# The first 60 microseconds of a transformer layer: vector work to GpSimd, loads in another order

## The chip, the core and the metric

The kernel runs on one core of a Trainium2 chip. The core has a matrix engine (TensorE, PE in the profile), a vector engine (VectorE, DVE), a scalar engine (ScalarE, ACT), a general engine (GpSimd, POOL) and a queue that issues the loads and stores (SyncE, SP). The metric is the device time of one execution in microseconds (us), and lower is better.

## The reference: one layer

One layer on a sequence of 1024 tokens of 1024 features. What matters here is the first product, `h = x @ w_in`, whose columns are cut into queries, keys, values and gates:

```python
h = x @ w_in[l]                       # (1024, 1024) @ (1024, 5120)
qa, ka, va, qb, kb, vb, ga, gb = jnp.split(h, split_pts, axis=-1)
y_a = chunk_band_attention(heads_a(qa), heads_a(ka), heads_a(va), rel_bias[l]) @ w_proj_a[l]
y_b = stick_breaking_attention(heads_b(qb), heads_b(kb), heads_b(vb)) @ w_proj_b[l]
mix = (gate_a * y_a + gate_b * y_b) @ w_out[l]
x = layer_norm(DEEPNORM_ALPHA * x + mix, ln1_g[l], ln1_b[l])
g, u = jnp.split(x @ w_ffn_in[l], 2, axis=-1)
x = layer_norm(DEEPNORM_ALPHA * x + (jax.nn.silu(g) * u) @ w_ffn_out[l], ln2_g[l], ln2_b[l])
```

All values are float32, and the result is held to float32 accuracy. The kernel reads x transposed (`xt`: features by tokens) and `w_in` cut into column blocks of 128, each stored as a 128 x 1024 tile.

## The kernel before

**Split operands.** A factor is cut into a high part, rounded to the matrix engine's fast float32 form (`F32R`), and a low part, the rest. A product takes three matmuls: high by high, high by low, low by high (`mm3`, line 112, and `product`, line 159). `split` (line 108) makes both parts: ScalarE casts the high part, VectorE subtracts it from the source for the low one. In the profile both stand at lines 109 and 110, whatever tile they make.

**Seven products for eight.** Two column blocks of weights, left and right, are projected together as a work unit. Unit 0 is done plainly (`project_plain`, line 301): four blocks of 24 matmuls, left and right weights by the first half of the tokens (columns `LO` of each x tile), then by the second (`HI`). Each block goes over the 8 x tiles. Later units use a Strassen-like scheme (`pair_steps`, line 174) of seven half-size products, 12 matmuls each, in the order p1, p2, p6, p5, p7, p3, p4. p1 and p2 read x's first half, p4 its second half, p6 and p3 the halves of the tiles `s24`, p5 and p7 the halves of `s13`. `s13` and `s24` are sums of parts of x (lines 266 to 275), made once for four pairs of x tiles (`kt` 0 to 3) and split themselves. The weights of a unit need combinations too: `prep_left` (line 128) loads and splits the left tile, `prep_right` (line 139) loads the right one, forms `ta` and `tb` and splits them, and `prep_last` (line 153) splits a half of the right one into the tile `c`.

**Order of the work.** `run_pairs` (line 377) first issues p1 and p2 of units 1 and 2, then the remaining five products of unit 1, and so on; weights of later units are prepared between. So on TensorE the beginning is: four plain blocks of unit 0, p1 and p2 of unit 1, p1 and p2 of unit 2, then p6, p5, p7, p3, p4 of unit 1.

**Before the first products** (lines 239 to 275) the left weights of unit 0 are loaded, then the first halves of the eight x tiles in the order 0, 4, 1, 5, 2, 6, 3, 7, and split; then the right weights of unit 0, two second halves of x, the left weights of unit 1, and the other six second halves. All subtractions and all sums are VectorE's. GpSimd has no work there but a few memsets.

**Buffers and queues.** Tiles have tags with a fixed number of buffers (`SLOTS`, line 43): three for raw weights (`gt`), four for scratch and sums (`kp`), eight for split weights (`op`). A tile that asks for a buffer in use waits for its last reader. All loads go through the one queue of SyncE. A planner at compile time ranks the instructions of each engine by their place in the program and by when it thinks that they are ready, so that the order on an engine can differ a little from the program's; once made, each engine's order is fixed, and the instructions wait on semaphores.

The steps that the prediction speaks of: `split` and `split_w` (lines 108, 133), `left`, `right` (lines 232, 235), the loads and splits (lines 239 to 265), the sums (266 to 275), `project_plain` (301), and `right(1)` at line 429.

Of the kernel before, what the change touches and what calls it, by code (L numbers as in the profile page):

```python
# [11 lines left out]
F32 = mybir.dt.float32  # L12
# [6 lines left out]
P = 128  # L19
# [28 lines left out]
def hybrid_trunk_kernel(ctx: ExitStack, tc, x, xt, w_in, b_gate, rel_bias, w_proj,  # L48
# [14 lines left out]
    def slot(tag, name, dtype=F32):  # L63
        return pool.tile([P, 1024], dtype, tag=tag, name=name, bufs=SLOTS[tag])
# [40 lines left out]
    s_dr = [[dram(f"s_dr{g}_{hf}_", 7) for hf in range(2)] for g in range(4)]  # L105
    rel_dr = dr.tile([8, 896], F32, name="rel_dr")

    def split(dst_h, dst_l, src):
        nc.scalar.copy(dst_h, src)  # L109
        nc.vector.tensor_tensor(dst_l, src, dst_h.bitcast(F32), ALU.subtract)  # L110

    def mm3(acc, pairs):
        n = len(pairs)
# [19 lines left out]
    def split_w(raw, nm, tag):  # L133
        h = slot(tag, f"{nm}h", F32R)
        l = slot(tag, f"{nm}l", F32R)
        split(h, l, raw)
        return h, l

    def prep_right(W, nm, src, tag, tag_a=None):
        sub = ALU.subtract  # L140
        L = W["L"]
        R = W["R"] = slot("gt", f"wR{nm}")
        dma(R, src)
        ta = slot("kp", f"ta{nm}")
        tb = slot("kp", f"tb{nm}")
        nc.vector.tensor_tensor(ta[:, LO], R[:, LO], L[:, LO], sub)
        nc.vector.tensor_tensor(tb[:, LO], R[:, HI], ta[:, LO], sub)
        nc.vector.tensor_tensor(tb[:, HI], L[:, HI], tb[:, LO], sub)
        W["hb"] = split_w(tb, f"wb{nm}", tag)
        nc.vector.tensor_tensor(ta[:, HI], R[:, HI], R[:, LO], sub)  # L150
        W["ha"] = split_w(ta, f"wa{nm}", tag_a or tag)

    def prep_last(W, nm, tag):

        c = slot(tag, f"wc{nm}", F32R)
        split(c[:, LO], c[:, HI], W["R"][:, HI])
        W["c"] = c
# [74 lines left out]
    def left(i):  # L232
        prep_left(Wa[i], f"p{i}", w_in[work[i][2]])

    def right(i):
        prep_right(Wa[i], f"p{i}", w_in[work[i][3]], "op")
        prep_last(Wa[i], f"p{i}", "kp")

    sops = {}
    s_tags = iter(["bw"] * 9 + ["pt"] * 4 + ["yt"] * 3)  # L240
    for kt in range(4):
        for nm in ("s24", "s13"):
            sops[nm, kt] = tuple(slot(next(s_tags), f"{nm}{p}{kt}", F32R) for p in "hl")
    order_k = [0, 4, 1, 5, 2, 6, 3, 7]
    xraw = [None] * KT
    for k in order_k:
        xraw[k] = cycle(QKV, f"xraw{k}")
    left(0)
    for k in order_k:
        dma(xraw[k][:, LO], xt[k * P:(k + 1) * P, LO])  # L250
    xh = [slot("xt", f"xh{k}", F32R) for k in range(KT)]
    xl = [slot("xt", f"xl{k}", F32R) for k in range(KT)]
    for k in order_k:
        split(xh[k][:, LO], xl[k][:, LO], xraw[k][:, LO])

    R0 = slot("gt", "wRp0")
    dma(R0, w_in[work[0][3]])
    Wa[0]["hr"] = split_w(R0, "wrp0", "op")
    for k in order_k[:2]:
        dma(xraw[k][:, HI], xt[k * P:(k + 1) * P, HI])  # L260
    left(1)
    for k in order_k[2:]:
        dma(xraw[k][:, HI], xt[k * P:(k + 1) * P, HI])
    for k in order_k:
        split(xh[k][:, HI], xl[k][:, HI], xraw[k][:, HI])
    for kt in range(4):
        a, b = xraw[kt], xraw[kt + 4]
        s13 = slot("kp", f"s13_{kt}")
        s24 = slot("kp", f"s24_{kt}")
        nc.vector.tensor_tensor(s13[:, LO], a[:, HI], b[:, HI], ALU.add)  # L270
        nc.vector.tensor_tensor(s24[:, LO], s13[:, LO], a[:, LO], ALU.subtract)
        nc.vector.tensor_tensor(s24[:, HI], b[:, LO], s24[:, LO], ALU.subtract)
        nc.vector.tensor_tensor(s13[:, HI], a[:, LO], a[:, HI], ALU.subtract)
        for src, nm in ((s24, "s24"), (s13, "s13")):
            split(*sops[nm, kt], src)

    def s_op(nm, half):
        return [tuple(t[:, half] for t in sops[nm, kt]) for kt in range(4)]
# [22 lines left out]
    def project_plain(i):  # L301

        W, pair = Wa[i], work[i][1]
        accs = {}
        for half in (LO, HI):
            for side, key in enumerate(("hl", "hr")):
                tag = "pv" if side and half == HI else "tr"
                acc = accs[side, half.start] = bank(tag, f"plain{side}_{half.start}")
                wh, wl = W[key]
                mm3(acc, [(wh[:, k * P:(k + 1) * P], wl[:, k * P:(k + 1) * P],  # L310
                           xh[k][:, half], xl[k][:, half]) for k in (0, 4, 1, 5, 2, 6, 3, 7)])
        def take():
            for side, (scale, d) in enumerate(((-0.125, q_dr), (1.0, k_dr))):
                h = cycle(QKV, f"hi{side}_{i}", F32R)
                t = cycle(QKV, f"lo{side}_{i}")
                for half in (LO, HI):
                    acc = accs[side, half.start]
                    nc.scalar.activation(h[:, half], acc, AF.Copy, scale=scale)
                    nc.vector.scalar_tensor_tensor(t[:, half], acc, scale,
                                                   h[:, half].bitcast(F32),  # L320
                                                   ALU.mult, ALU.subtract)
                store_hl(d[pair], h, t)
        return take
# [102 lines left out]

    left(2)
    take = project_plain(0)
    right(1)
    take()  # L430
    run_pairs([project(i) for i in range(1, len(work))], lambda i: left(i + 1) if i > 1 else None,
              lambda i: right(i + 1), lambda i: small_inputs() if i == 2 else None)
# [692 lines left out]
```

## Time and profile before

| | us |
|---|---|
| median of three runs | 1466.01 |
| lowest and highest of them | 1466.0 and 1467.67 |
| the profiled execution's own time | 1465.81 |
| its span (first to last instruction) | 1464.0 |
| TensorE busy in the span | 1432.2 |
| VectorE busy | 1025.3 |
| ScalarE busy | 679.4 |
| GpSimd busy | 278.1 |

A row of the timeline has the start and the length in us, the engine, the line of the kernel, the operation, the tile written and those read, the shape, and in brackets the idle time of the engine before it and what ended that. A row of the groups has, behind the bar, the busy time in us and the mean length of one instruction in ns. Instructions on one engine overlap a little at their ends: the row of a 512-wide VectorE instruction is 0.69 us long, but the next one starts 0.60 us after it.

### The profile page before, as it was taken

How to read it: one execution, taken by the hardware profiler on the slowest of the kernel's cores; microseconds unless marked ns; L12 is line 12 of the kernel's file. 1: busy time of each engine (PE TensorE's matmuls, PEld its weight loads, DVE VectorE, ACT ScalarE, POOL GpSimd, SP SyncE). 2: the span in 40 equal slices, each digit the busy share in tenths (PEclk: the TensorE clock that was granted, in tenths of full speed). 3: DMA queues.
4: the chain of work that ended last, by engine and by line, in shares of the span. 5: the costliest groups of instructions: out<-in, count | busy, mean ns of one | idle time of the engine just before them, and what ended most of it. 6: DMA issues, size and time to landing. Idle time of an engine off the chain costs nothing.

```text
span 1464.0 us, 19115 instructions
## 1 busy us (share of the span) xinstructions
PE 1432.2 (98%) x6740; PEld 1184.4 (81%) x6740; DVE 1025.3 (70%) x1637; ACT 679.4 (46%) x1179; POOL 278.1 (19%) x326
## 2 busy tenths in 40 slices
PE   8999999999999998999999999999999999999997
PEld 6788888887888787878888888888888888888886
DVE  8856655434776876887848966777776665978767
ACT  6444444335878878775413534444444433221201
POOL 0000000003555879760004100000000000100016
PEclk9999999999999999999999999999999999999999
DMA  6565545338666476856611123444444457887602
GB/s 216 158 188 173 157 145 177 124 99 249 188 196 206 131 217 184 238 179 247 232 43 72 50 95 130 158 154 148 152 151 145 152 195 247 301 308 235 213 15 101
DMA packets 83455, 247.72 MB, mean 169 GB/s; under 512 B 10512, under 2 KB 10512, under 8 KB 83360
## 3 DMA queue, kind: packets, MB, share of 16 engines
q1 hardware_dynamic: 83360, 246.51, 51.5%
q8 instruction: 53, 0.87, 0.3%
q14 instruction: 42, 0.34, 0.1%
HBM read 162.03 MB, written 80.77 MB: 166 GB/s over the span
## 4 chain that ended last, share of the span: by engine, by line
PE 86%; DVE 5%; DMA 3%; ACT 3%; issue 2%; POOL 1%; SPq 0%; POOLq 0%; DVEq 0%; ACTq 0%
PE sxf L171 16%; PE sxp L171 12%; PE szf L171 8%; PE dx L1058 6%; PE szp L171 6%; PE syf L171 4%; PE gps L421 3%; PE dz L1058 3%; PE syp L171 3%; PE yAps L630 2%; PE ops L117 2%; PE ops L119 2%; PE ops L116 2%; PE fpswh_h L119 1%; PE fpswh_h L116 1%
## 5 line engine op out<-in xcount | busy, mean ns | idle before, releaser
L1014 POOL TENSOR_TENSOR wdyt<-wdyt 128x512 f32<-128x512 f32 x8 | 10.8, 1352 | 513.6 <-DMA wdgt<-in_w_ffn_out_dram 429.1
L547 POOL TENSOR_TENSOR w_b<-w_b,kp_b 128x511 f32<-128x511 f32 (+3 forms) x96 | 96.2, 1010 | 39.0 <-DVE kp_b L542 27.0
L542 DVE TENSOR_TENSOR_SCAN kp_b<-kp_b,ident_ps 128x512 f32<-128x512 f32 (+2 forms) x64 | 56.4, 883 | 24.8 <-ACT kp_b L539 24.3
L482 POOL MEMSET bias<- 64x64 f32 x8 | 1.2, 144 | 329.7 <-ACT bias L481 329.7
L778 POOL TENSOR_TENSOR mv<-mv,neghalf 128x1 f32<-128x1 f32 x16 | 23.8, 1489 | 210.3 <-DVE mv L777 210.3
L184 DVE TENSOR_TENSOR c<-sxp,c 128x512 f32<-128x512 f32 x16 | 11.1, 691 | 74.2 <-issue 41.1
L539 ACT ACTIVATE kp_b<-sc_b 128x512 f32<-128x512 f32 (+3 forms) x96 | 50.0, 521 | 24.9 <-PE sc_b L465 23.2
L110 DVE TENSOR_TENSOR pt_b<-tp_b,pt_b 128x512 fp32r<-128x512 f32 (+1 forms) x96 | 50.4, 543 | 13.8 <-ACT pt_b L109 13.5
L989 DVE TENSOR_TENSOR x<-dx,x 128x512 f32<-128x512 f32 x64 | 43.5, 686 | 17.0 <-PE dx L1058 16.9
L171 PE MATMUL szf<-x1S63h,wcf 128*128 128x512 f32 x168 | 55.1, 389 | 0.0
L109 ACT CAST pt_b<-tp_b 128x512 fp32r<-128x512 f32 (+1 forms) x96 | 48.2, 515 | 7.7 <-PE tp_b L570 6.1
L110 DVE TENSOR_TENSOR sl<-h,sl 128x512 fp32r<-128x512 f32 x56 | 38.4, 685 | 18.8 <-ACT sl L109 18.8
L512 POOL TENSOR_SCALAR w_a<-w_a,st_a 128x640 f32<-128x640 f32 (+2 forms) x64 | 42.6, 670 | 45.1 <-DVE st_a L511 33.5
L109 ACT CAST sl<-h 128x512 fp32r<-128x512 f32 x56 | 34.7, 619 | 34.5 <-PE syf L171 17.1
L110 DVE TENSOR_TENSOR pt_a<-tp_a,pt_a 128x512 fp32r<-128x512 f32 (+1 forms) x96 | 45.8, 486 | 6.8 <-ACT pt_a L109 5.5
L540 ACT ACTIVATE w_b<-sc_b 128x511 f32<-128x511 f32 (+3 forms) x96 | 50.2, 523 | 0.0
L570 PE MATMUL tp_b<-ident,w_b 128*128 128x128 f32 x288 | 48.7, 279 | 1.5 <-DVE pt_b L110 1.1
L116 PE MATMUL ops<-wh_o,mh 128*128 128x512 f32 x128 | 50.2, 392 | 0.0
L119 PE MATMUL ops<-wh_o,ml 128*128 128x512 f32 x128 | 50.0, 391 | 0.0
L117 PE MATMUL ops<-wl_o,mh 128*128 128x512 f32 x128 | 49.9, 390 | 0.0
L109 ACT CAST pt_a<-tp_a 128x512 fp32r<-128x512 f32 (+1 forms) x96 | 39.7, 426 | 19.2 <-PE tp_a L570 17.8
L507 ACT ACTIVATE w_a<-w_a,st_a 128x640 f32<-128x640 f32 (+2 forms) x64 | 44.7, 698 | 6.4 <-DVE st_a L501 5.9
(1883 smaller groups left out, 4811.4 us busy)
## 6 DMA issues: line engine op xcount, KB each, us to landing
s_dr<-sl SPq DMA_DIRECT2D x112, 256.0 KB, 2.1
sd<-s_dr SPq DMA_DIRECT2D x56, 512.0 KB, 4.5
wLf<-in_w_ffn_in_dram SPq DMA_DIRECT2D x22, 512.0 KB, 4.3
wRf<-in_w_ffn_in_dram SPq DMA_DIRECT2D x22, 512.0 KB, 3.6
wLp<-in_w_in_dram SPq DMA_DIRECT2D x17, 512.0 KB, 5.4
wRp<-in_w_in_dram SPq DMA_DIRECT2D x17, 512.0 KB, 4.2
v_dr<-v SPq DMA_DIRECT2D x16, 512.0 KB, 4.6
qs<-q_dr SPq DMA_DIRECT2D x16, 512.0 KB, 5.3
```

Source lines behind the costliest of these rows:

```text
L109: nc.scalar.copy(dst_h, src)
L110: nc.vector.tensor_tensor(dst_l, src, dst_h.bitcast(F32), ALU.subtract)
L116: mm(acc, lh, rh, start=(i == 0), stop=False)
L117: mm(acc, lh, rl, start=False, stop=False)
L119: mm(acc, ll, rh, start=False, stop=(i == n))
L171: mm(acc, lw[:, ks], rx, start=(first and kt == i == 0), stop=(kt == 3 and i == 2), skip_group_check=not first)
L539: nc.scalar.activation(kp[:, c0:e], sc[:, 0:n], AF.Sigmoid, scale=-1.0)
L540: nc.scalar.activation(be[:, m0:e], sc[:, m0 - c0:n], AF.Sigmoid)
L542: nc.vector.tensor_tensor_scan(kp[:, 0:e], kp[:, 0:e], ident_ps()[:, 0:e], 0.0, ALU.mult, ALU.add)
L547: nc.gpsimd.tensor_tensor(be[:, m0:e], be[:, m0:e], kp[:, m0 - 1:e - 1], ALU.mult)
L570: tr(tp[:, (qb - lo_q) * P:(qb - lo_q + 1) * P], wt[qb - q0][:, (kb - qb) * P:(kb - qb + 1) * P], ident)
L1058: mm(acc, a, b, start=(first and i == n == 0), stop=(i == n - 1 == 1), skip_group_check=not first)
```

## The change

It touches the beginning and the helpers that it uses.

1. `split` can be given the engine that subtracts. `right` can leave its last step, the tile `c`, to a new `right_last`.
2. TensorE multiplies a tile of zeros five times (128 x 256, float32) into a bank that nothing reads, ahead of everything else.
3. The left weights of unit 0 come in two halves, the first ahead of x's first two tiles, the second behind them. x's first half comes in the order 0 to 7, and `project_plain` takes the tiles in that order for the first half of the tokens.
4. The right weights of unit 0 come ahead of x's whole second half, and the left and right weights of unit 1 behind it. The right weights are split in halves: the low part of the first half on VectorE, of the second half on GpSimd.
5. The low parts of x's second half are all GpSimd's (8 instructions of 128 x 512).
6. Of each `s13` and `s24` the first halves stay VectorE's, and the second halves, sums and low parts, go to GpSimd (4 instructions of 128 x 512 for each `kt`). Splits of these tiles are made by halves, so ScalarE has two casts for each one before.
7. The combinations of unit 1's right weights (`right(1, False)`) stand ahead of the sums in the program; before they stood behind the first products. The tile `c` stays behind them.

```diff
-    def split(dst_h, dst_l, src):
+    def split(dst_h, dst_l, src, eng=None):
         nc.scalar.copy(dst_h, src)
-        nc.vector.tensor_tensor(dst_l, src, dst_h.bitcast(F32), ALU.subtract)
+        (eng or nc.vector).tensor_tensor(dst_l, src, dst_h.bitcast(F32), ALU.subtract)
...
-    def right(i):
+    def right(i, last=True):
         prep_right(Wa[i], f"p{i}", w_in[work[i][3]], "op")
+        if last:
+            right_last(i)
+
+    def right_last(i):
         prep_last(Wa[i], f"p{i}", "kp")
...
     order_k = [0, 4, 1, 5, 2, 6, 3, 7]
+    warm = cst.tile([P, 256], F32, name="warm")
+    nc.vector.memset(warm, 0.0)
+    warm_ps = bank("mm", "warm")
+    for _ in range(5):
+        mm(warm_ps[:, 0:256], warm[:, 0:P], warm, start=True, stop=True)
+
     xraw = [None] * KT
     for k in order_k:
         xraw[k] = cycle(QKV, f"xraw{k}")
-    left(0)
-    for k in order_k:
-        dma(xraw[k][:, LO], xt[k * P:(k + 1) * P, LO])
     xh = [slot("xt", f"xh{k}", F32R) for k in range(KT)]
     xl = [slot("xt", f"xl{k}", F32R) for k in range(KT)]
+    L0, R0 = slot("gt", "wLp0"), slot("gt", "wRp0")
+    for key, t in (("hl", L0), ("hr", R0)):
+        Wa[0][key] = slot("op", f"w{key}h", F32R), slot("op", f"w{key}l", F32R)
+
+    def x_in(ks, cs):
+        for k in ks:
+            dma(xraw[k][:, cs], xt[k * P:(k + 1) * P, cs])
+
+    dma(L0[:, LO], w_in[work[0][2]][:, LO])
+    x_in((0, 1), LO)
+    dma(L0[:, HI], w_in[work[0][2]][:, HI])
+    x_in(range(2, 8), LO)
+    dma(R0, w_in[work[0][3]])
+    x_in(order_k, HI)
+    for ks, cs in ((range(4), LO), (range(4, 8), HI)):
+        split(*(t[:, cs] for t in Wa[0]["hl"]), L0[:, cs])
+        for k in ks:
+            split(xh[k][:, LO], xl[k][:, LO], xraw[k][:, LO])
+    for cs, eng in ((LO, nc.vector), (HI, nc.gpsimd)):
+        split(*(t[:, cs] for t in Wa[0]["hr"]), R0[:, cs], eng)
     for k in order_k:
-        split(xh[k][:, LO], xl[k][:, LO], xraw[k][:, LO])
-
-    R0 = slot("gt", "wRp0")
-    dma(R0, w_in[work[0][3]])
-    Wa[0]["hr"] = split_w(R0, "wrp0", "op")
-    for k in order_k[:2]:
-        dma(xraw[k][:, HI], xt[k * P:(k + 1) * P, HI])
+        split(xh[k][:, HI], xl[k][:, HI], xraw[k][:, HI], nc.gpsimd)
     left(1)
-    for k in order_k[2:]:
-        dma(xraw[k][:, HI], xt[k * P:(k + 1) * P, HI])
-    for k in order_k:
-        split(xh[k][:, HI], xl[k][:, HI], xraw[k][:, HI])
+    right(1, False)
+    put = nc.vector.tensor_tensor
+    put2 = nc.gpsimd.tensor_tensor
     for kt in range(4):
         a, b = xraw[kt], xraw[kt + 4]
         s13 = slot("kp", f"s13_{kt}")
         s24 = slot("kp", f"s24_{kt}")
-        nc.vector.tensor_tensor(s13[:, LO], a[:, HI], b[:, HI], ALU.add)
-        nc.vector.tensor_tensor(s24[:, LO], s13[:, LO], a[:, LO], ALU.subtract)
-        nc.vector.tensor_tensor(s24[:, HI], b[:, LO], s24[:, LO], ALU.subtract)
-        nc.vector.tensor_tensor(s13[:, HI], a[:, LO], a[:, HI], ALU.subtract)
-        for src, nm in ((s24, "s24"), (s13, "s13")):
-            split(*sops[nm, kt], src)
+        put(s13[:, LO], a[:, HI], b[:, HI], ALU.add)
+        put(s24[:, LO], s13[:, LO], a[:, LO], ALU.subtract)
+        put2(s24[:, HI], b[:, LO], s24[:, LO], ALU.subtract)
+        put2(s13[:, HI], a[:, LO], a[:, HI], ALU.subtract)
+        for nm, src, cs, eng in (("s24", s24, LO, nc.vector), ("s13", s13, LO, nc.vector),
+                                 ("s13", s13, HI, nc.gpsimd), ("s24", s24, HI, nc.gpsimd)):
+            split(*(t[:, cs] for t in sops[nm, kt]), src[:, cs], eng)
...
-                           xh[k][:, half], xl[k][:, half]) for k in (0, 4, 1, 5, 2, 6, 3, 7)])
+                           xh[k][:, half], xl[k][:, half])
+                          for k in (range(KT) if half == LO else order_k)])
...
-    right(1)
+    right_last(1)
     take()
```

## The prediction

> **What bounds the kernel now.** I read the page first (busy shares), then the chain of waits in the first 75 us, then the timelines of TensorE, VectorE and GpSimd there, and last GpSimd's rows late in the kernel, because the early trace does not show what the change asks of GpSimd. Page:
>
> ```profile
> span 1464.0 us, 19115 instructions
> PE 1432.2 (98%) x6740; PEld 1184.4 (81%) x6740; DVE 1025.3 (70%) x1637; ACT 679.4 (46%) x1179; POOL 278.1 (19%) x326
> ```
>
> TensorE (PE) is the bound and is idle for 1464.0 - 1432.2 = 31.8 us in all. So a change of the beginning can win only what TensorE waits or runs slowly there, and any delay there stays, since TensorE has almost nothing later in which to catch up. TensorE's timeline, each row with its wait in brackets:
>
> ```profile
> 5.81 0.80 PE L116 MATMUL plain<-xh,wlp0h 128*128 128x512 f32 x1 [5.81 <-ACT xh L109]
> 12.01 0.63 PE L116 MATMUL plain<-xh,wlp0h 128*128 128x512 f32 x1
> 12.44 0.63 PE L117 MATMUL plain<-xl,wlp0h 128*128 128x512 f32 x1
> 13.20 0.40 PE L116 MATMUL plain<-xh,wlp0h 128*128 128x512 f32 x1
> 13.43 0.40 PE L117 MATMUL plain<-xl,wlp0h 128*128 128x512 f32 x1
> 15.28 0.39 PE L116 MATMUL plain<-xh,wrp0h 128*128 128x512 f32 x1
> 20.74 0.39 PE L116 MATMUL plain<-xh,wlp0h 128*128 128x512 f32 x1
> 26.18 0.39 PE L116 MATMUL plain<-xh,wrp0h 128*128 128x512 f32 x1
> 44.25 0.50 PE L171 MATMUL sxp<-s24h,wbp1h 128*128 128x512 f32 x1 [0.93 <-ACT wbp1h L109]
> 45.51 0.50 PE L171 MATMUL sxp<-s24h,wbp1l 128*128 128x512 f32 x1 [0.53 <-DVE wbp1l L110]
> 48.74 0.50 PE L171 MATMUL sxp<-s13h,wap1h 128*128 128x512 f32 x1 [0.68 <-ACT c L197]
> 57.04 0.39 PE L171 MATMUL sxp<-xh,wbp1h 128*128 128x512 f32 x1
> ```
>
> The four plain blocks of 24 matmuls (left and right weights with x's first half, then with its second) start at 5.81, 15.28, 20.74 and 26.18. Until 12.44 the matmuls start 0.43 us apart (12.44 - 12.01), after that 0.23 (13.43 - 13.20): the half-speed start. A full-speed block takes 5.45 us (20.74 - 15.28), the first took 9.47. The product of work unit 1 that reads the last sum (p3) ends at 57.04; that time is my yardstick. The chain of waits (start, length, who) shows what sets the time between the plain blocks and there:
>
> ```profile
> 18.36 0.68 DVE xl L110
> 24.45 0.60 DVE s L271
> 25.06 1.14 DVE s24l L110
> 42.44 0.68 DVE tbp L148
> 44.26 1.20 DVE wbp1l L110
> 45.51 2.58 PE sxp L171 x10
> ```
>
> From 18.36 to 45.5 the chain is nearly all VectorE (DVE). The view by stages (stretch, its length, then busy us and count of PE, PEld, DVE, ACT, POOL) has it full and GpSimd (POOL) empty:
>
> ```profile
> 30.00:35.00 5.00, 5.00 (x23) 4.13 (x22) 5.00 (x8) 2.35 (x3) 0.00 (x0) 1.00 0.41 86
> ```
>
> Its 512-wide instruction costs 0.60 us, its 1024-wide one 1.14. The three waits at 44.25 to 48.74 (0.93 + 0.53 + 0.68 = 2.1 us) are its price so far.
>
> **The change part by part.** *Loads.* The bytes are the same, in another order. The rows of the scalar engine (ACT) that end on a landing:
>
> ```profile
> 8.99 3.33 ACT L109 CAST xh<-xraw 128x512 fp32r<-128x512 f32 x5 [0.69 <-DMA xraw<-in_xt_dram]
> 12.98 1.05 ACT L109 CAST wrp0h<-wRp 128x1024 fp32r<-128x1024 f32 x1 [0.66 <-DMA wRp<-in_w_in_dram]
> 15.62 1.05 ACT L109 CAST wlp1h<-wLp 128x1024 fp32r<-128x1024 f32 x1 [0.55 <-DMA wLp<-in_w_in_dram]
> ```
>
> The right weights land at 12.98 behind the left ones and x's first half, and do so again. Between 12.98 and 15.62, four pieces of 256 KB (two of x, one left weight) landed, 0.66 us each. After the change x's second half comes from 13.6 to about 18.3, unit 1's left weights at about 19.6 and its right ones at 20.9 (before: left at 15.62). On the DMA queue (SP) unit 2's left weights now wait for the right weights' buffer, which GpSimd's subtract frees at about 16; they are needed after 36, so this costs nothing unless they came 14 us late.
>
> *Weights in halves and zeros first.* The first cast is half as long and the first load 256 KB instead of 512, so the first real matmul can start near 4.9 instead of 5.81. The zero matmuls have no row before. By the count of columns five of 256 cost at least 5 x 0.21 = 1.1 us (half of 0.43), at most 5 x 1.12 = 5.6 (twice 0.279 for a 128-wide float32 transpose, twice again for the half-speed clock):
>
> ```profile
> L570 PE MATMUL tp_b<-ident,w_b 128*128 128x128 f32 x288 | 48.7, 279 | 1.5 <-DVE pt_b L110 1.1
> ```
>
> ```profile
> 0.71 0.20 POOL masks.py:197 MEMSET ident<- 128x128 f32 x1 [0.29 <-POOLq L1115]
> ```
>
> A memset stands ahead of them; with the first such rows at 0.71 I start them at 1.2, and they end between 2.3 and 6.8. I take 4.6 (five of 0.169 x 4; 0.169 is the group's busy time over its count, scaled in the same way): in time. If they run to 6.8, block 1 starts 2 us later but still meets the next limit. That limit is the last piece of x's first half: the five casts from 8.99 end at 12.32, its subtract follows at about 12.9, its last matmuls at 13.4. The right weights' first half is cast by 13.6. So block 2 starts at about 13.7 instead of 15.28, and this part gains 1.6 us at most, nothing if the clock stays low (8 x 3 x 0.43 = 10.3 us from 4.9 is 15.2). [...]
>
> *Half of the vector work to GpSimd.* This decides. Moved are 25 subtracts of 128x512: 1 of the right weights, 8 lows of x's second half, and per sum tile pair 4 (two sums, two lows) x 4. VectorE loses 25 x 0.60 = 15 us. All 25 read two SBUF operands, and so does nearly everything that VectorE keeps here. GpSimd's queue is empty in this stretch, so nothing of its own stands behind them; VectorE's queue does. ACT gets ten 1024-wide casts as twenty 512-wide ones, 10 x (2 x 3.33/5 - 1.05) = 2.8 us over some 45 us, in which it is about half idle: nothing. How VectorE and GpSimd stand beside each other is shown late in the trace, at lines 1014 and 110:
>
> ```profile
> 1244.85 1.29 POOL L1014 TENSOR_TENSOR wdyt<-wdyt 128x512 f32<-128x512 f32 x1 [9.07 <-PE fpswh_h L119]
> 1303.67 1.63 POOL L1014 TENSOR_TENSOR wdyt<-wdyt 128x512 f32<-128x512 f32 x1 [14.66 <-DVE wdgt L1013]
> ```
>
> ```profile
> 1244.63 0.68 DVE L1072 SCALAR_TENSOR_TENSOR x<-x,fpswh_h 128x512 f32<-128x512 f32 x1
> 1245.22 1.45 DVE L110 TENSOR_TENSOR wdc<-wdyt,wdc 128x512 fp32r<-128x512 f32 x1
> 1303.45 0.69 DVE L110 TENSOR_TENSOR wdc<-wdyt,wdc 128x512 fp32r<-128x512 f32 x1
> ```
>
> VectorE's subtract of two SBUF tiles that began during GpSimd's took 1.45 us instead of 0.69, and ended at 1246.67, 0.53 after GpSimd's end at 1246.14. In the other order GpSimd took 1.63 instead of 1.29 and ended at 1305.30, 1.16 after VectorE's end at 1304.14. The instruction with a PSUM operand (1244.63) was not held. So such instructions go one at a time: a GpSimd one holds the pair for 1.16, a VectorE one for 0.53 to 0.60, and 25 moved instructions add 25 x 1.16 = 29.0 to what 25 x 0.60 = 15.0 took before. [...]
>
> *The sum.* From 13.6, when the first half of the right weights is cast, until p3's last matmuls, the pair must do: VectorE 22 of 0.60 (1 right weights, 4 of unit 1's combinations, 16 of the sums, 1 of its last weights) and 4 of 1.14 (low parts of three of unit 1's weights and of unit 2's left ones) = 17.8; GpSimd 29.0. Together 46.8, so the last low part is written at 60.4 at the earliest, and p3 ends 0.45 later (two matmuls), at 60.9 against 57.04: +3.9 us. VectorE's four PSUM evictions (2.4 us) run beside GpSimd and cost nothing; without that cover 2.4 us more.
>
> The order adds to that. Taking turns, GpSimd's first nine end at 14.1 + 9 x 1.16 + VectorE's turns between (7 of 0.53, 2 of 1.07) = 30.4. The third block needs the ninth and ends at about 30.9 instead of 26.18, so 4.7 late. Then 72 matmuls (16.3 us) run to 47.2 (p6; before 44.25). The sums of the last tile pair take scratch buffers (tag kp, four of them) that GpSimd's seventeenth instruction frees at 30.4 + 8 x 1.69 = 43.9; its four VectorE instructions at a turn of 1.69 each, its casts (0.67 twice), and what stands ahead of them (1.14, 0.60, evictions 2.4) end at 43.9 + 6.8 + 1.3 + 4.1 = 56.1. Product p5 needs that, and behind it p5's last three matmuls, p7 and p3 take 0.7 + 2.7 + 2.7 = 6.1: p3 ends at 62.2 if no turn is lost; one or two lost pairs (1.69 each) put it at 64 or 66. I take 63.0, or +6.0. From there TensorE has its order as before and nothing to catch up with. The profiled execution took 1465.81 us (span 1464.0 and 1.8 around it), 0.2 under the median of 1466.01; 1465.8 + 6.0 = 1471.8, so 1472.
>
> **Rivals.** *The engines run beside each other* (the other side). If the wait at line 110 came from something else, GpSimd's nine end at 14.1 + 9 x 1.29 = 25.7, block 3 at 26.2; behind it 24 + 48 + 48 matmuls of 0.227 (27.2) run with no wait, since 16 more GpSimd instructions (20.6 us) are done at 46.3, before p7 at 48. p3 ends at 53.4: -3.6, and 1462. For it: VectorE sets the chain now. Against it: the rows above, in both orders. It decides if VectorE's subtracts beside GpSimd stay under about 0.75 us.
>
> *One engine keeps the pair while it has work.* The rows show single meetings only, not who is next. If GpSimd goes first, its nine are in time, but VectorE's low halves come last: they end at 60.4, and 6.1 of matmuls follow: 66.5, +9.5, 1475. With idle turns in it (VectorE waiting for GpSimd's buffers and the reverse) five more: 1480. If VectorE goes first, block 3 ends near 35 (13.6 + 9 x 1.16 + 4.8 + 1.1 + 4.7 of its ready work + 0.5) and p3 at 35.1 + 27.2 = 62.3: inside my forecast.
>
> *The pair is shared but enough is hidden*: the floor of +3.9 less the 1.0 to 2.0 that instructions of both engines overlap at their ends (a VectorE's stand 0.60 apart but hold 0.53: 22 x 0.07 = 1.5), so +1.9 to +2.9: 1468, no change that can be told.
>
> **How the numbers follow.** About 0.2% (2.9 us) can be told from no change. Chances: taking turns or a like order, +3 to +8: 0.59; one engine keeping the pair, above +8: 0.20; hidden, within 2.9 either way: 0.13; beside each other, faster by over 2.9: 0.08. So faster 0.08, same 0.13, slower 0.79. The range leaves out the gain and part of the middle case below and the tail of the idle turns above: 1466 to 1480.
>
> **What the profile after would show.** Right: VectorE's subtracts between 14 and 60 us last 1.2 to 1.9 us instead of 0.69, GpSimd is busy from 14 to about 60, block 2 starts near 13.7, block 3 ends near 31 with waits for GpSimd's xl, and TensorE waits again before p5 or p7, for sums. Matmuls 0.23 us apart from the first on show the zeros right. Wrong: VectorE's rows at 0.69 beside a busy GpSimd, or a p3 that ends before 57. What would also spoil it: another order of VectorE's instructions, since the order in the program is made by a planner that ranks what it thinks is ready; a wait that this moves to a later stage is not in my sum.

## The result, and the profile after

The changed kernel takes 1479.32 us (median of five runs, 1477.76 to 1481.09) where the kernel before takes 1466.01: a ratio of 1.0093, 95% interval 1.0080 to 1.0107, so 13.3 us slower. The forecast was 1472.0, 6 us slower: right in its direction, and short by half of the loss. The profiled execution took 1477.76 us, 1.6 under the median.

From the page of the kernel after, its span and the busy time of each engine:

```profile
span 1476.0 us, 19171 instructions
PE 1434.5 (97%) x6750; PEld 1185.8 (80%) x6750; DVE 1028.3 (70%) x1623; ACT 680.0 (46%) x1189; POOL 319.0 (22%) x351
```

TensorE is idle for 1476.0 - 1434.5 = 41.5 us instead of 31.8. That is 9.7 of the 12.0 us by which the span grew; the other 2.3 are busy time, the net of the zeros (4.6 us, where TensorE was idle before), of matmuls that ran slowly and of others that ran faster. TensorE's timeline shows both (start, length, what is multiplied; in brackets the idle time before and what ended it):

```profile
8.07 0.50 PE L116 MATMUL plain<-xh,whlh 128*128 128x512 f32 x1 [1.57 <-ACT xh L109]
...
15.14 0.39 PE L116 MATMUL plain<-xh,whrh 128*128 128x512 f32 x1
...
27.09 0.50 PE L117 MATMUL plain<-xl,whlh 128*128 128x512 f32 x1 [0.72 <-POOL xl L110]
27.65 0.40 PE L116 MATMUL plain<-xh,whrh 128*128 128x512 f32 x1
...
41.43 0.50 PE L171 MATMUL sxp<-xh,wlp2l 128*128 128x512 f32 x1 [2.25 <-DVE wlp2l L110]
...
56.22 0.80 PE L171 MATMUL sxp<-s24h,wbp1h 128*128 128x512 f32 x1 [9.50 <-ACT c L188]
60.96 0.39 PE L171 MATMUL szp<-s13h,wap1h 128*128 128x512 f32 x1
63.70 0.39 PE L171 MATMUL sxp<-s13h,wap1h 128*128 128x512 f32 x1
66.42 0.39 PE L171 MATMUL szp<-s24h,wcp 128*128 128x512 f32 x1
...
69.14 0.39 PE L171 MATMUL sxp<-xh,wbp1h 128*128 128x512 f32 x1
```

Block 2 starts at 15.14 (before 15.28), block 3 ends at 27.65 (before 26.18), p1 of unit 2 waits 2.25 us for the low part of its left weights (before 0.37), and then p6 of unit 1 stands still for 9.50 us. It starts at 56.22, p5 at 60.96, p7 at 63.70, p3 at 66.42, and p3 ends at 69.14 against 57.04: 12.1 us late. Up to about 300 us TensorE stays 12.1 us behind. From there to 720 us the lag moves: of two later products, `sc_b` starts at 482.10 against 468.11, 13.99 late, and `yBps` at 686.26 against 675.42, 10.84 late. The clock falls to half for 3.4 to 6.8 us there, at 374 us in this execution, at 576 and 655 in the one of before. From 720 us on the lag is 11.8. That 12.1 and the span's 12.0 agree so well is therefore in part chance.

The p6 row names as its releaser not a sum but `c L188`, ScalarE's copy of p1's result out of PSUM, the memory in whose banks TensorE leaves its sums. Such a copy or add that reads a result out of its bank is called an eviction below. The chain of waits (start, length, who) shows what that copy stood behind:

```profile
51.09 1.74 DVE s L291
...
52.86 0.61 ACT s24h L109
...
53.50 0.62 ACT wcp L109
54.12 1.04 ACT s13h L109 x2
55.16 0.52 ACT s24h L109
55.68 0.49 ACT c L188
...
56.22 4.91 PE sxp L171 x12
```

The last tile pair's sum (VectorE, line 291) ends at 52.83; behind it, in ScalarE's queue, come five casts of 512 columns, and only then the copy. In the kernel before the same two copies, for units 1 and 2, stood elsewhere. ScalarE's timeline of before, and then of after:

```profile
35.16 0.57 ACT L188 COPY c<-sxp 128x512 f32<-128x512 f32 x1
...
44.10 0.58 ACT L188 COPY c<-sxp 128x512 f32<-128x512 f32 x1
```

```profile
55.59 1.06 ACT L188 COPY c<-sxp 128x512 f32<-128x512 f32 x2
```

The copies were 20.4 and 12 us later. The view by stages (stretch, length, busy us and count of PE, PEld, DVE, ACT, POOL, then TensorE's clock) shows the second part of the loss, the clock, and how full the pair VectorE and GpSimd was:

```profile
15.00:20.00 5.00, 5.00 (x24) 4.14 (x23) 0.00 (x0) 4.12 (x7) 5.00 (x5) 1.00 1.04 405
...
45.00:50.00 5.00, 1.71 (x8) 1.09 (x6) 4.94 (x3) 3.05 (x6) 4.92 (x4) 1.00 0.41 107
50.00:55.00 5.00, 0.00 (x0) 0.00 (x0) 3.91 (x4) 2.15 (x5) 4.38 (x4) 0.51 0.00 0
55.00:60.00 5.00, 3.78 (x9) 3.04 (x10) 5.00 (x6) 1.65 (x4) 4.61 (x3) 0.50 0.41 105
```

While TensorE stood still, its clock fell to half (0.51, 0.50). In the records of the clock the half-speed stretch goes from 50.06 to 60.30, so p6 ran in it and took 4.74 us (56.22 to 60.96) instead of the 2.72 of p7 and p3. VectorE and GpSimd are both about 5.00 busy from 45 to 50, but only three VectorE instructions fall in that stretch. Their timelines, VectorE first:

```profile
20.43 2.09 DVE L110 TENSOR_TENSOR wlp1l<-wLp,wlp1h 128x1024 fp32r<-128x1024 f32 x1 [6.43 <-ACT wlp1h L109]
...
46.52 1.75 DVE L290 TENSOR_TENSOR s<-xraw,xraw 128x512 f32<-128x512 f32 x1
48.19 1.75 DVE L110 TENSOR_TENSOR s24l<-s,s24h 128x512 fp32r<-128x512 f32 x1
...
56.70 1.76 DVE L110 TENSOR_TENSOR s13l<-s,s13h 128x512 fp32r<-128x512 f32 x1
...
59.58 1.27 DVE L184 TENSOR_TENSOR c<-syp,c 128x512 f32<-128x512 f32 x2
```

```profile
15.13 11.90 POOL L110 TENSOR_TENSOR xl<-xraw,xh 128x512 fp32r<-128x512 f32 x8
...
46.12 1.60 POOL L293 TENSOR_TENSOR s<-xraw 128x512 f32<-128x512 f32 x1
47.68 1.71 POOL L292 TENSOR_TENSOR s<-xraw,s 128x512 f32<-128x512 f32 x1
...
57.87 1.73 POOL L110 TENSOR_TENSOR s24l<-s,s24h 128x512 fp32r<-128x512 f32 x1
```

Where both had work that reads two tiles of SBUF (the memory that holds the tiles), from 46.1 to 49.9 and from 52.9 to 59.6, they start alternately, each about 1.7 us after its own last: turns, as forecast. The last rows of VectorE are the end of its sums (58.46) and behind them its adds of p2's results (line 184). At the start there were few turns: VectorE stood idle for 6.43 us until 20.43 (0.00 busy from 15 to 20), waiting for unit 1's left weights, which the prediction itself had landing at about 19.6, and GpSimd's eight `xl` took 11.90 us, 1.49 each. GpSimd's last instruction ends at 59.60; the forecast had 60.4.

### The profile page after: what moved, and what is told of

It reads as the page before. It is cut to its first block, busy times and chain, and to the rows that moved or that the text cites. A ratio compares the mean times of both kernels' runs of the same rounds, so it can differ in the third digit from the quotient of the medians.

```text
span 1476.0 us, 19171 instructions
## 1 busy us (share of the span) xinstructions
PE 1434.5 (97%) x6750; PEld 1185.8 (80%) x6750; DVE 1028.3 (70%) x1623; ACT 680.0 (46%) x1189; POOL 319.0 (22%) x351
## 4 chain that ended last, share of the span: by engine, by line
PE 86%; DVE 4%; DMA 3%; ACT 3%; POOL 2%; issue 1%; SPq 0%; POOLq 0%; DVEq 0%; ACTq 0%
PE sxf L171 15%; PE sxp L171 12%; PE szf L171 8%; PE dx L1080 6%; PE szp L171 6%; PE syf L171 4%; PE gps L443 3%; PE dz L1080 3%; PE syp L171 3%; PE yAps L652 2%; PE tp_b L592 2%; PE ops L117 2%; PE ops L119 2%; PE ops L116 2%; PE fpswh_h L119 1%; PE fpswh_h L117 1%
## 5 line engine op out<-in xcount | busy, mean ns | idle before, releaser
L117 PE MATMUL ops<-wl_o,mh 128*128 128x512 f32 x128 | 49.9, 390 | 0.0
```

What stands on the lines that cost most here:

```text
L117: mm(acc, lh, rl, start=False, stop=False)
```

## The experiments

Each kernel was timed beside the kernel before on the same chip (its median there 1465.2 to 1466.2 us); "+4.1" is the difference of the two medians. A trace is of one execution; where that one lay more than 3 us from its kernel's median, the text says so.

### 1. All 25 instructions back on VectorE, the rest as changed

```diff
-        (eng or nc.vector).tensor_tensor(dst_l, src, dst_h.bitcast(F32), ALU.subtract)
+        nc.vector.tensor_tensor(dst_l, src, dst_h.bitcast(F32), ALU.subtract)
...
-    put2 = nc.gpsimd.tensor_tensor
+    put2 = nc.vector.tensor_tensor
```

> The changed kernel with its 25 GpSimd instructions given back to VectorE; loads, halves and zeros stay as changed. Theory (GpSimd and VectorE exclude each other, and that makes the loss): the loss goes; VectorE's subtracts are 0.69 us again, unit 1's p3 ends between 55 and 58 us, and the time is 1463 to 1467. Rival (the other parts of the change, the order of loads or unit 1's weights ahead of the sums, make the loss): 1472 or more.

Measured: 1469.49 us (1467.6 to 1474.85), ratio 1.0029 [1.0017, 1.0042], +4.1. Neither number came. GpSimd's part is 9 to 10 us of the 13.3 (1479.3 - 1469.5 = 9.8, or 13.3 - 4.1 = 9.2), and something in the rest costs 2.5 to 6 us by the interval. The forecast had nothing for that rest. The trace is of the slowest of the ten executions, 1474.85 us; p3 ends there at 63.38.

### 2. Only the 25 instructions moved, the rest as before

```diff
-        split(xh[k][:, HI], xl[k][:, HI], xraw[k][:, HI])
+        split(xh[k][:, HI], xl[k][:, HI], xraw[k][:, HI], nc.gpsimd)
...
+        nc.gpsimd.tensor_tensor(s24[:, HI], b[:, LO], s24[:, LO], ALU.subtract)
+        nc.gpsimd.tensor_tensor(s13[:, HI], a[:, LO], a[:, HI], ALU.subtract)
+        for nm, src, cs, eng in (("s24", s24, LO, nc.vector), ("s13", s13, LO, nc.vector),
+                                 ("s13", s13, HI, nc.gpsimd), ("s24", s24, HI, nc.gpsimd)):
```

> The kernel before with nothing changed but the 25 instructions that go to GpSimd (the second half of the right weights, x's second half, the second halves of the sums); loads in the old order, no zeros. Theory (exclusion): p3 ends 6 to 13 us later than the 57.0 of the kernel before, the time is 1472 to 1480. Rival (the new order of the loads makes the loss): 1464 to 1468.

Measured: 1485.3 us (1484.06 to 1487.53), ratio 1.0134 [1.0119, 1.0149], +19.9: worse than the whole change, and 5 us above the theory's range. GpSimd's timeline in this kernel shows why:

```profile
19.37 1.74 POOL L110 TENSOR_TENSOR xl<-xraw,xh 128x512 fp32r<-128x512 f32 x1
21.07 2.27 POOL L274 TENSOR_TENSOR s<-xraw,s 128x512 f32<-128x512 f32 x1
23.32 1.71 POOL L275 TENSOR_TENSOR s<-xraw 128x512 f32<-128x512 f32 x1
24.99 5.86 POOL L110 TENSOR_TENSOR xl<-xraw,xh 128x512 fp32r<-128x512 f32 x4
```

The planner put sums (lines 274, 275) between the low parts of x that block 3 waits for. In this kernel block 3 runs from 22.20 to 37.29 with waits of 2.81 and 1.96 us for GpSimd's `xl`, much of it at half clock (27.36 to 41.01 by the records of the clock), and p6 waits 4.50 us more; p3 ends near 74.6. In the changed kernel unit 1's combinations stand ahead of the sums, and the eight `xl` ran in one piece, from 15.13 to 27.03. So the change's new order (which part of it, no run shows) protected GpSimd's first nine, while it cost elsewhere (experiment 6).

### 3. GpSimd only writing

```diff
+    def fill(dst):
+        for _ in range(FILLS):
+            nc.gpsimd.memset(dst, 0.0)
...
-            (eng or nc.vector).tensor_tensor(dst_l, src, dst_h.bitcast(F32), ALU.subtract)
+            fill(dst_l.bitcast(F32))
...
-        put2(s24[:, HI], b[:, LO], s24[:, LO], ALU.subtract)
-        put2(s13[:, HI], a[:, LO], a[:, HI], ALU.subtract)
+        fill(s24[:, HI])
+        fill(s13[:, HI])
```

> The changed kernel with each of GpSimd's 25 subtracts replaced by two memsets of the same 128x512 target, which read nothing; the low parts and sums that it made are left out (zeros stand there). Theory (the two engines exclude each other only where both read two SBUF tiles or read SBUF): VectorE's rows beside a busy GpSimd are 0.69 us, p3 ends at 53 to 57 us, and the time is 1462 to 1466. Rival (VectorE is slowed by any work of GpSimd, or the loss lies in waiting for GpSimd's results and in the order of the queues): VectorE's rows stay at 1.7, or p3 ends after 60 and the time is 1470 or more.

Measured: 1461.36 us (1460.72 to 1463.44), ratio 0.9975 [0.9962, 0.9987], -4.0. VectorE's timeline, and GpSimd's beside it:

```profile
28.67 0.69 DVE L116 TENSOR_TENSOR s13l<-s,s13h 128x512 fp32r<-128x512 f32 x1
```

```profile
28.01 0.53 POOL L111 MEMSET s<- 128x512 f32 x1
28.48 0.53 POOL L111 MEMSET s13l<- 128x512 f32 x1
```

VectorE's subtract of two SBUF tiles takes 0.69 us beside a GpSimd that only writes, against 1.75 above beside one that reads. So it is not a busy GpSimd as such that slows VectorE here, but one that subtracts SBUF tiles. With the turns gone p3 ends at 53.64, where the prediction's rival "beside each other" had 53.4, and the time is its 1462 within a microsecond. Exclusion and the latency of GpSimd's results together are worth 1479.3 - 1461.4 = 18 us. They are not apart here: a memset also waits for no cast. Those of `xl` were done before 13 us, so that GpSimd was busy for 12.4 us between 13 and 60 against 39.6 in the changed kernel; what VectorE's rows show is the stretch from 27 to 34 us, where GpSimd was busy for 6.74.

### 4. p6 of unit 1 in a bank of its own

```diff
-            product(st["sx"], W, ops, 6, False)
+            if nm == "p1":
+                begin("sx", "tr", 6)
+            else:
+                product(st["sx"], W, ops, 6, False)
```

> The changed kernel, but unit 1's p6 starts a PSUM bank of its own instead of adding to p1's, so that it doesn't wait until ScalarE has copied p1 out; p1's part of two of unit 1's results is left out. Theory (the copy stands in ScalarE's queue behind the last casts of the sums, and that wait, 9.5 us and a slower clock behind it, is what I missed): p6 starts near 46 us instead of 56.2, waits inside for the last sums, and p3 ends at 63 to 65 instead of 69.1; the time falls by 4 to 6 us to about 1473 to 1475. Rival (p6 waits for the sums all the same): p3 ends at 68 to 69 and the time is 1477 to 1479.

Measured: 1479.95 us (1475.84 to 1483.45), ratio 1.0095 [1.0073, 1.0117], +14.6. The theory that ScalarE's copy alone holds the chain has fallen; p3 ends at 69.85, as late as in the changed kernel. The traced execution, 1475.84 us, is the fastest of the four. TensorE's timeline in this kernel:

```profile
49.66 0.50 PE L171 MATMUL sxp<-s24l,wbp1h 128*128 128x512 f32 x1 [1.72 <-DVE s24l L110]
53.22 0.80 PE L171 MATMUL sxp<-s24h,wbp1h 128*128 128x512 f32 x1 [2.83 <-ACT s24h L109]
...
60.02 0.80 PE L171 MATMUL szp<-s13h,wap1h 128*128 128x512 f32 x1 [3.94 <-DVE c L184]
```

p6 no longer waited for the copy and began at 46.20, but it ran in pieces as the sums came, and p5 then waited 3.94 us for VectorE's add at line 184 (p2's result), which stands behind the sums on VectorE as the copy does on ScalarE. The two evictions and the sums themselves all end between 56 and 60; taking away one leaves the next.

### 5. Only the first nine on GpSimd, the sums on VectorE

```diff
-    put2 = nc.gpsimd.tensor_tensor
+    put2 = nc.vector.tensor_tensor
...
-                                 ("s13", s13, HI, nc.gpsimd), ("s24", s24, HI, nc.gpsimd)):
+                                 ("s13", s13, HI, nc.vector), ("s24", s24, HI, nc.vector)):
```

> The changed kernel with only the first nine instructions on GpSimd (the right weights' second half and the low parts of x's second half); the sixteen of the sums are VectorE's again. Theory (each moved instruction costs the pair about 0.56 us net, 1.16 for 0.60, while VectorE is the chain): between the kernel with none on GpSimd (1469.5) and the changed one (1479.3), by count about 1473; 1471 to 1476. Rival (the nine lie where VectorE has nothing to do and cost nothing): 1468 to 1470.

Measured: 1474.11 us (1472.74 to 1475.79), ratio 1.0062 [1.0046, 1.0078], +7.9, as the theory had it. Against experiment 1 that is about 0.5 us for each instruction moved ((1474.1 - 1469.5) / 9), near the forecast's 1.16 - 0.60; over all 25 it is 9.8 / 25 = 0.39.

### 6. All on VectorE, and unit 1's right weights late as before; zeros alone

```diff
-    right(1, False)
...
-    right_last(1)
+    right(1)
```

> As the kernel with all vector work on VectorE, but unit 1's right weights are loaded and combined behind the plain products again, as before the change; loads of x and unit 0, halves and zeros stay as changed. Theory (what still costs 4 us there is that unit 1's combinations stand ahead of the sums and hold up ScalarE's copies of p1, behind which p6 waits): 1463 to 1466.5. Rival (the new order of x and unit 0's weights, or the split of the sums into halves, costs it): 1468 to 1471.

Measured: 1466.91 us (1464.11 to 1468.85), ratio 1.0003 [0.9992, 1.0014]. So the 3 to 4 us of experiment 1 are the combinations of unit 1's right weights ahead of the sums, and the loads in halves, their order and the zeros together are worth nothing that can be told. The theory was 0.4 us low, and it had only half of the mechanism: with the right weights early p6 waits 3.14 us for ScalarE's copy, with them late 1.63 us for its own weights. The larger difference is at unit 2's left weights. VectorE's row of their low part, in experiment 1 and then here:

```profile
47.85 1.22 DVE L110 TENSOR_TENSOR wlp2l<-wLp,wlp2h 128x1024 fp32r<-128x1024 f32 x1
```

```profile
37.30 1.22 DVE L110 TENSOR_TENSOR wlp2l<-wLp,wlp2h 128x1024 fp32r<-128x1024 f32 x1
```

With the right weights early, these are cast at 32.98 instead of 23.40, their low part stands behind most of the sums, and unit 2's p1 goes on at 49.12 instead of 38.58.

The kernel before with the zeros alone:

```diff
+    for _ in range(5):
+        mm(warm_ps[:, 0:256], warm[:, 0:P], warm, start=True, stop=True)
```

> The kernel before with the five zero products ahead of it and nothing else. Theory (the clock rises early but falls again in the gaps between the first loads of x, as in the changed kernel, and what block 1 gains is lost again in the waits before p6): 1464.5 to 1466.5, no difference that can be told. Rival (block 1 at full clock throughout, gain kept): 1461 to 1463.5.

Measured: 1467.12 us (1463.56 to 1470.41), ratio 1.0013 [1.0001, 1.0025]: no gain, rather a loss of 0.9 us. Its view by stages, of the slowest of the ten executions (TensorE's clock is the number behind the five engines):

```profile
5.00:10.00 5.00, 3.19 (x8) 1.45 (x8) 3.34 (x5) 2.56 (x6) 0.00 (x0) 0.91 0.89 277
10.00:15.00 5.00, 5.00 (x18) 3.95 (x18) 4.37 (x7) 4.16 (x7) 0.00 (x0) 0.75 1.04 407
```

The zeros did raise the clock, to full at 5.65 us by its records, but TensorE was busy for 3.19 of the next 5 us only, and from 9.06 to 12.48 the clock was at half again, just when x had come.

### 7. Evictions ahead of the last tile pair's sums

The function given as `then` is called behind p1 and p2 of units 1 and 2.

```diff
-    for kt in range(4):
+    def sums(kt):
...
+    for kt in range(3):
+        sums(kt)
...
+              then=lambda: sums(3))
```

> The changed kernel with all 25 on GpSimd, but the sums of the last tile pair stand behind p1 and p2 of units 1 and 2 in the program, so that ScalarE's and VectorE's copies of p1 and p2 out of PSUM stand ahead of them in their queues. Theory (p6 and p5 need the banks that these copies free, and the copies queue behind all sums; this is what put p5, p7 and p3 wholly behind the end of the shared work): p6 starts before 50 us, p3 ends at 63 to 66 instead of 69.1, time 1473 to 1476. Rival (the sums alone set it): p3 ends at 68 to 70, time 1478 to 1481.

Measured: 1475.96 us (1474.49 to 1476.32), ratio 1.0072 [1.0057, 1.0087], +9.8 instead of +13.3. p6 starts at 50.92 instead of 56.22 and still waits 2.61 us for the copy; p3 ends at 66.57 instead of 69.14. The theory's time came, p3 half a microsecond later than it said. The place of the evictions behind the last sums is therefore worth 3.5 us, about half of the 7.3 that the forecast lacked, and not all of the wait is gone.

### 8. Towards a faster version: the early sums first, in four steps

From here on everything stays on VectorE. First, the low halves of the sums of all four tile pairs (those that p6 and p5 read) come first, one scratch tile for each pair; the high halves of pairs 1 to 3 and unit 0's stores (`take`) stand behind p1 and p2 of units 1 and 2.

```diff
+    left(2)
+    for kt in range(4):
+        sums_lo(kt)
+    sums_hi(0)
...
+    def rest():
+        for kt in range(1, 4):
+            sums_hi(kt)
+        take()
...
+              lambda i: right(i + 1), lambda i: small_inputs() if i == 2 else None, then=rest)
```

> All vector work on VectorE; loads, halves and zeros as changed; of the sums the low halves (which p6 and p5 read) of all four tile pairs come first, the high halves (p7 and p3) of the last three behind p1 and p2 of units 1 and 2, and with them the copies of the plain products; unit 2's left weights ahead of the sums. Theory (what TensorE waits for before p6 is the order on VectorE, not the sum of its work): p6 starts at 42 to 43 us with no wait over 0.5, p3 ends at 53 to 55 against 57.0 before the change, time 2 to 4 us under the kernel before, 1462 to 1464. Rival (VectorE's work as a whole sets it): p6 starts after 44, p3 ends at 56 or later, 1465 to 1468.

Measured: 1468.06 us (1463.18 to 1473.59), ratio 1.0014 [1.0004, 1.0025], +2.8: a miss. The trace is of the slowest of the twelve executions, 1473.59 us. p6 and p5 wait for nothing now, but the wait stands before p7 (TensorE's timeline):

```profile
53.95 0.79 PE L171 MATMUL sxp<-s13h,wap1h 128*128 128x512 f32 x1 [3.97 <-ACT c L197]
```

Next, eight matmuls on data already there fill TensorE's early waits, six behind x tile 0 and two behind tile 1 of block 1, into the bank that nothing reads:

```diff
+            for _ in range(fill[i - 1] if i <= len(fill) else 0):
+                mm(warm_ps, lh, rh, start=True, stop=True)
...
+                    [6, 2] if half == LO and side == 0 else [])
```

> As the one with the low halves first, and six and two repeated matmuls (into the bank that nothing reads) behind the first and second x tile of block 1, where TensorE waits for loads. Theory (the clock falls because TensorE is idle there): all matmuls of block 1 are 0.23 us apart, block 2 starts at 13.2 to 14.2 instead of 15.1, p3 ends at 51 to 53.5, time 1460 to 1462.5. Rival (the clock falls or p6 waits all the same): block 2 starts at 14.8 or later or the time equals that of the one with the low halves first.

Measured: 1465.73 us (1463.61 to 1469.93), ratio 1.0005 [0.9995, 1.0016]. The clock is full from 5.12 to 49.49 us, and block 2 starts at 13.89 instead of 15.14 in the changed kernel. That part of the theory came, its time did not: p7 waits again, and p3 ends at 58.82 (the traced execution took 1468.95 us, 3.2 over the median). TensorE's timeline, and ScalarE's:

```profile
50.57 0.80 PE L173 MATMUL sxp<-s13h,wap1h 128*128 128x512 f32 x1 [3.88 <-ACT c L199]
```

```profile
48.22 0.62 ACT L109 CAST s24h<-s 128x512 fp32r<-128x512 f32 x1 [0.52 <-DVE s L299]
49.42 0.62 ACT L109 CAST s13h<-s 128x512 fp32r<-128x512 f32 x1 [0.58 <-DVE s L300]
49.94 0.58 ACT L199 COPY c<-sxp 128x512 f32<-128x512 f32 x1
```

It is the pattern of the changed kernel once more: the copy of p6's result stands behind the casts of the last sums. So the third step puts p6, and the tile of its result, ahead of the last pair's high halves:

```diff
+        tile_for[1]("2")
...
+    def p6_then_rest():
+        p6_of_1()
+        sums_hi(3)
+        take()
```

> As the kernel of the sums' low halves first with the repeated matmuls, but unit 1's p6 stands ahead of the last tile pair's high halves of the sums in the program, and its temporary tile is taken before that pair gives its buffers back; ScalarE's copy of p6's result thereby stands six places earlier in its queue. Theory (p7's wait of 3.88 us was for that copy, which stood behind the casts of the last sums and needed a buffer that they held): p7 starts at 46.5 to 47.5 us after a wait under 1 us, p3 ends at 52 to 54.5, the time is 1459.5 to 1462.5 us, 3 to 6 us under before. Rival (the high halves of the sums themselves, on VectorE, set p7): p7's wait stays at 3 us or more, p3 ends at 57 or later, 1464 to 1467 us.

Measured: 1466.01 us (1462.37 to 1468.42), ratio 1.0006 [0.9997, 1.0016]. p7's wait is gone (it starts at 46.62) and p3 ends at 52.33 (54.94 less the wait below), both as the theory said; the time is the rival's all the same, because the next product waits in its place, for VectorE's add of p7. TensorE's timeline, and VectorE's:

```profile
54.94 0.50 PE L173 MATMUL sxp<-xh,wbp1h 128*128 128x512 f32 x1 [2.61 <-DVE c L186]
```

```profile
51.20 1.28 DVE L353 SCALAR_TENSOR_TENSOR lo<-plain,hi 128x512 f32<-128x512 f32 x2
52.40 0.68 DVE L148 TENSOR_TENSOR tap<-wRp,wLp 128x512 f32<-128x512 f32 x1
...
54.20 0.68 DVE L186 TENSOR_TENSOR c<-sxp,c 128x512 f32<-128x512 f32 x1
```

The add at 54.20 stands behind unit 0's stores (line 353) and unit 2's combinations, none of which TensorE needs yet. The fourth step moves these two behind it:

```diff
-                if j == 0 and i + 1 < n:
+                if j == (2 if i == 0 else 0) and i + 1 < n:
                     right(i + 1)
...
-        take()
...
+              lambda i: take() if i == 0 else small_inputs() if i == 2 else None, then=rest)
```

> As the kernel with ScalarE's copy ahead, but the combinations of unit 2's right weights stand behind unit 1's p7 instead of its p6, and the stores of unit 0's blocks (four VectorE and four ScalarE instructions on 512 columns) behind unit 1's p4. Theory (p4's wait of 2.61 us was VectorE's add of p7 standing behind four combinations and four instructions of those stores, 8 x 0.60 = 4.8 us): p4 of unit 1 starts at 51.5 to 53 us with a wait under 1 us, p6 of unit 2 at 55 to 56.5 (59.4 without the move), and the time is 1460 to 1463.5 us. Rival (VectorE's sum of work sets the beginning, and any order only moves the wait to the next product): a wait of 2 us or more before a product of unit 2 or 3, unit 3's first product at 74 or later, 1464.5 to 1467 us.

Measured: 1463.92 us (1459.03 to 1465.52), ratio 0.9988 [0.9977, 0.9999]: the first of these four under the kernel before, by 1.5 us. The interval just excludes no change, and the gain is smaller than the 0.2% from which on, by the prediction, a change can be told. p4 of unit 1 starts at 53.44 after a wait of 1.07 us, p6 of unit 2 at 56.29, and no product of unit 2 or 3 waits, so the rival fell; p4's start and the time are a little over the theory's (53 and 1463.5 at most). The lead lasts: the first matmul of unit 3's p4, in TensorE's timeline of this kernel and then of before:

```profile
88.15 0.39 PE L173 MATMUL sxp<-xh,wbp3h 128*128 128x512 f32 x1
```

```profile
91.71 0.39 PE L171 MATMUL sxp<-xh,wbp3h 128*128 128x512 f32 x1
```

That is 3.56 us earlier, of which the medians show 1.5 and the two profiled executions 3.0 (1462.76 against 1465.81). Between the two traces the lead shrinks and grows again between 300 and 720 us, as the lag of the changed kernel did; why the medians show so much less was not followed up.

## Why the prediction was right and wrong

**What bounds the kernel: right, to 2 or 3 us.** A delay of p3's end was to stay, and it did: 12.1 us at p3's end, 12.0 in the span. The yardstick is not finer than that, since what follows after 300 us moves: in the trace with the right weights late (experiment 6) p3 ends 2.4 us late, at 59.45, and that execution is only 0.5 us longer than the profiled one of before.

**The pair goes in turns: right.** VectorE's rows were to last 1.2 to 1.9 us; most of those that met GpSimd's last 1.64 to 1.78. The sum of the pair's work was to end at 60.4 and ended at 59.60, the 6.43 us of VectorE's idle time included. Experiment 3 takes the turns away and lands on the rival's 53.4. GpSimd's first nine were to end at 30.4 and ended at 27.03: VectorE was idle beside them, so few turns were taken. Block 3 ended at 27.65 instead of 30.9.

**The step that failed** is "Product p5 needs that, and behind it p5's last three matmuls, p7 and p3 take 0.7 + 2.7 + 2.7 = 6.1". "That" are the last tile pair's low halves, which the forecast had ready at 56.1. VectorE's last of them ended at 58.46 (row 56.70). With 6.1 us behind it p3 would have ended near 64.6, an estimate; it ended at 69.14, so 10.7 us were left at that point and not 6.1. For p6 had started only at 56.22, and p6 (4.74 us at half clock), p5, p7 and p3 (2.74 + 2.72 + 2.72) took 12.9 from there. That p6 started so near the forecast's 56.1 is chance, for what ended there was ScalarE's copy and not a sum. The forecast let p6 start at 47.2, directly behind the matmuls before it. It did not look at what the products need besides operands: p6 adds onto p1's sum in its PSUM bank, so ScalarE's copy of p1 must come first, and p5 needs a bank that VectorE's add of p2 frees. Both instructions stand in the queues of the two engines that make the sums, behind the last pair's. The row `ACT L188`, at 35.16 before, was there to be read. Experiments 4, 7 and the steps of 8 show it: one eviction freed alone gains nothing, since the other and the sums end as late; evictions ahead of the last sums give back 3.5 us; and in each later version the next wait was again for an eviction behind sums or other vector work.

**From nothing to 3.4 us: the right weights ahead of the sums.** The forecast costed the combinations' new place at nothing beside their share of the sum, and of unit 2's left weights it said that their delay "costs nothing unless they came 14 us late". With everything on VectorE the place costs 1469.5 against 1466.9, and those weights hold unit 2's p1 until 49.12 instead of 38.58; with GpSimd's part the same wait is 2.25 us (row 41.43). The ladder, each against its own runs of before, is +0.7 (loads, halves, zeros), +4.1 (with the combinations early), +7.9 (with the nine on GpSimd) and +13.3 (with the sums there too): 0.7, 3.4, 3.8 and 5.4 us for the four parts, each known to 2 or 3 us only.

**Zeros and first loads: "this part gains 1.6 us at most, nothing if the clock stays low".** It gained 0.14 us in this pair of traces (15.14 against 15.28). The clock rose by 5.7 us and fell again at 9.10, behind the 1.57 us that TensorE waited for x tile 1 (row 8.07): a case between the two that the forecast named. In the trace of experiment 4, whose beginning is the same, that wait was 1.11 us, the clock stayed full and block 2 started at 13.01. So the gain is there in some executions; by the medians the beginning as a whole is worth nothing that can be told (experiment 6).

**The rivals.** "One engine keeps the pair" has the right time (1475 to 1480) by the wrong mechanism: the engines take turns, and it is the queue behind the last sums that makes the products late. "Hidden" and "beside each other" fell with the rows of 1.75 us.

## What to carry to other kernels

When work is moved between engines, list what a late product needs besides its operands: the buffer or bank that it writes, and the instruction that empties it. If that instruction stands in the queue of an engine that also makes the operands, the product starts when the last operand is made, whatever part of it could start earlier (here p6 at 56.22 us, after a wait of 9.50); write evictions ahead of work that is not ready. VectorE and GpSimd, which here took turns at work that reads two SBUF tiles, gained nothing from sharing a list of it: each instruction moved cost 0.4 to 0.5 us instead of saving 0.6.

## What the runs showed of the hardware

- Where VectorE and GpSimd both had work that reads two SBUF tiles, they took turns: for 3.8 and 6.7 us at a time in the changed kernel (46.1 to 49.9, 52.9 to 59.6) both start every 1.7 us. The memsets on GpSimd in experiment 3 (0.53 us for 128x512) took no part in them (VectorE's rows stay at 0.69).
- The long wait of the changed kernel cost a second time by the clock. In the wait of 9.50 us, which began at 46.72, TensorE's clock fell to half for 10.24 us, 50.06 to 60.30, and p6 lost 2.0 us by it. In the traces of experiments 1 and 5, where p6 waited too (3.14 us in experiment 1), matmuls stand 0.43 us apart as well, from 49.72 to 51.85 and from 50.24 to 54.08, and 0.23 to 0.24 behind that.
- With the zeros alone, raising the clock early gained most in the trace where TensorE then waited least. Eight traces have this beginning (the changed kernel, experiments 1, 3, 4, 5, the right weights late in 6, experiment 7, and the first of 8): block 2 starts between 13.01 and 17.18 in them. The clock stayed full where TensorE waited 1.11 us for x tile 1 (block 2 at 13.01), and fell to half where it waited 1.33 to 2.93 us (block 2 at 14.65 to 17.18; before the change at 15.28). With eight more matmuls in the early waits the clock stayed full, and block 2 starts at 13.89 and 13.72 in the traces of the second and the fourth step of 8.
